# A planner's order chosen in forty rounds, zeros products in planned pauses, and kb sums copied out of PSUM

## The chip, the cores and the metric

The kernel runs on one core of one Trainium2 chip. The metric is the device time of one execution in microseconds (us). TensorE multiplies matrices, VectorE and ScalarE work element by element, GpSimd (POOL in the profile) does small jobs, SyncE (SP) issues nearly all DMAs. TensorE reads SBUF and writes PSUM, which has eight banks of 128 partitions x 512 fp32.

## The reference

Two layers (DEPTH = 2) of a decoder trunk on x of 256 tokens x 1024 channels, in fp32:

```
ada = silu(c) @ w_ada[l] + b_ada[l]                 # 6 x 1024: shift, scale, gate, twice
h   = rms_norm(x) * (1 + sc_m) + sh_m
q_a, kc, vc, ks, vs, kw, vw, g, q_b, k_b, v_b, g_br = split(h @ w_in[l])
y_a = nsa_mixer(...)      # 8 heads: compressed, selected and window attention, gated
y_b = moba_mixer(...)     # 8 heads, causal attention in blocks of 256
x  += g_m * ((sig(g_br_a) * (y_a @ w_up_nsa) + sig(g_br_b) * (y_b @ w_up_moba)) @ w_out)
h   = rms_norm(x) * (1 + sc_f) + sh_f
x  += g_f * ((silu(h @ w_gate) * (h @ w_up)) @ w_ffn_out)
```

The weights come to some 180 MB that are each read once. With 256 tokens all blocks are selected, so both mixers are causal attention beside the compressed branch.

## The kernel before, in words

**Number form.** Most weights are split on the chip: a raw block of 1 MB is landed by one DMA, ScalarE copies it to float32r (`hi`, line 444), VectorE computes `lo = raw - hi` (line 396), and TensorE does three products (x_hi w_hi, x_hi w_lo, x_lo w_hi) of 512 columns each (`mm3`, line 461). Some blocks stay whole and are multiplied in fp32. Tokens are two tiles of 128 (t = 0, 1). A sum of 512 output columns takes one PSUM bank; `dense` sums over two weight blocks into banks of the kind `acc`, of which there are three, and then calls a function that reads the sum from the bank (`post_qa`, `post_qb`, `post_kb`, `post_vb`). `post_kb` squares the sum on ScalarE, reduces the squares on VectorE, multiplies the sum by two rope tables on VectorE (each reading the bank), normalises with a power on GpSimd, and transposes.

**Stages.** The lead-in streams w_ada rows (`sa`) and w_in rows side by side, eight steps of k, while PE waits for each step's modulation. Then in each layer: `post_grpA` and the compressed branch `mlp`, q, k and v sums, attention (`nsa`, `moba`), four gate blocks, up-projections, w_out, the residual and norm of each t (`h_chain`), and the FFN.

**Modulation.** Apart from the lead-in the 80 rows of w_ada that are left (0.5 MB each, tile `aw`, three buffers) are loaded between the weights: `ada_pace(n)` is called with every weight load and draws n rows on average. Each row costs one dot product on VectorE (line 402). `ADA_PACE` holds three paces for each layer: from mlp on, from the third gate block on, in the FFN.

**The order.** Nothing is issued as it is written. Every operation becomes an `Op` with a cost for each engine that may do it; buffers are `Slot`s of a `Kind`, handed out in the order of first use. `levels` gives each op the length of the longest path behind it. `order` then simulates the engines: in each step it takes the engine that can start first and, of the ops that could start within a small window (`eps`), the one of the highest rank (level, plus a boost, plus 1000 for ops made under `R.ahead()`). DMAs are modelled at 385 bytes a ns plus 2 us. `emit` issues the instructions of all engines in that order; on the chip each engine runs its own instructions in that order and waits for semaphores. The clock of TensorE is not in the model.

Of the kernel before, what the change touches and what calls it, by code (L numbers as in the profile page):

```python
# [16 lines left out]
P = 128  # L17
# [23 lines left out]
class Cell:  # L41
    def __init__(self):
        self.busy, self.free_at = False, 0.0
# [67 lines left out]
class Op:  # L111
    def __init__(self, no, alts, key):
# [5 lines left out]
        self.func, self.loads = None, None  # L118
# [5 lines left out]
FIRST = 1000.0  # L124
LAT = {"PE": 0.24, "DVE": 0.09, "ACT": 0.09, "POOL": 0.2, "SP": 0.0, "Q": 0.0}
# [5 lines left out]
class Program:  # L131
    WAIT = 1.0
    BIAS = {"DVE": 0.8, "POOL": 0.5}
# [77 lines left out]
    def levels(self):  # L211
        for op in self.ops:
            for p in op.preds.values():
                p.succs.append(op)
# [20 lines left out]
    def order(self):  # L235
# [3 lines left out]
        for k in self.kinds.values():  # L239
            k.queue = deque(sorted((v for v in k.queue if v.ops), key=lambda v: v.first.no))  # L240
            for v in k.queue:
                v.left = v.ops
# [8 lines left out]
        ends = {}  # L251
        table = ()

        def place(op):
# [5 lines left out]
            for v in op.new:  # L260
                k = v.kind
                i = taken.get(id(k), 0)
                if len(k.queue) <= i or k.queue[i] is not v:
                    return None
                taken[id(k)] = i + 1
# [19 lines left out]
        while len(out) < len(self.ops):  # L285
# [4 lines left out]
            for op in ready:  # L290
# [5 lines left out]
                for e, (c, _) in op.alts.items():  # L296
                    est = max(free[e], pl[0],
                              max((f if q == e else f + LAT[q] for f, q in rt[op.no].values()), default=0.0))
                    per.setdefault(e, []).append((est, op, pl[1], c))
            self.done, self.ready = out, ready  # L300
            assert per, "stuck"
            for e, cs in per.items():
# [3 lines left out]
                else:  # L306
                    pick = max((c for c in cs if c[0] <= t0 + eps[e]), key=lambda c: (c[1].rank(e), -c[1].no))
# [9 lines left out]
            if len(op.alts) > 1:  # L317
# [4 lines left out]
                t = done[e] - c  # L322
            for v, s in zip(op.new, picks):
                v.kind.queue.popleft()
                v.slot, v.placed = s, True
                for cell in s.cells:
                    cell.busy = True
            if op.loads is not None:
# [15 lines left out]
            for v in op.acc:  # L344
                v.left -= 1
                v.end = max(v.end, end + LAT[e])
                if v.left == 0:
                    for cell in v.slot.cells:
                        cell.busy, cell.free_at = False, v.end
# [13 lines left out]

    def emit(self):
        for t, e, op in self.order():
# [6 lines left out]
class Engines:  # L372
# [83 lines left out]
    def mm(self, out, lhsT, rhs, start, stop, cost=None):  # L456
        if cost is None:
# [3 lines left out]
        self.p.op({"PE": (cost, [lambda: self.nc.tensor.matmul(AP(out), AP(lhsT), AP(rhs), start=start, stop=stop)])},  # L461
                  [lhsT, rhs], [out])
# [4 lines left out]
    def dma(self, out, src, q="SP"):  # L467
        o = AP(out)
        n = SIZE[o.dtype]
        for d in o.shape:  # L470
# [3 lines left out]
                  [src], [out], nbytes=max(n, 60000))  # L474
# [7 lines left out]
ADA_PACE = [(0.4, 2.5, 1.0), (0.4, 1.2, 0.6)]  # L482
# [11 lines left out]
def trunk_kernel(tc, pools, A):  # L494
# [27 lines left out]
    bc = [[Cell()] for _ in range(8)]  # L522
    for kind, ids in (("acc", (0, 1, 2)), ("s", (3, 4)), ("y", (5,)), ("t", (6, 7)), ("n", (0, 1, 2, 3, 4, 5))):
# [63 lines left out]
    zb = const("zb", [P, P], BF16)  # L587
# [33 lines left out]
    def ada_rows(l, kind, k, col):  # L621
        aw = R.val("aw")
        dma(aw, A["w_ada"][l, kind * D + k * P:kind * D + (k + 1) * P])
        ada_dot(aw, col)

    def ada_all():
        for l, nm in ((0, "g_m"), (0, "f"), (0, "g_f"), (1, "m"), (1, "g_m"), (1, "f"), (1, "g_f")):
            mod, _ = ada_tiles(l)
            if nm in ("m", "f"):
                kind = {"m": 0, "f": 3}[nm]  # L630
                for k in range(KD):
                    for j in range(2):
                        ada_rows(l, kind + j, k, mod[kind].of((j, k))[:, j, k:k + 1])
                        if (k, j) == (KD - 1, 1):
                            ada_mod(l, kind, slice(0, KD))
                        yield
# [11 lines left out]
    ada_due = [0.0]  # L648

# [16 lines left out]
    def ada_pace(n):  # L666
        ada_due[0] += n
# [67 lines left out]
    def h_rstd(t, log):  # L735
# [16 lines left out]
        else:  # L752
            ts(r, s1, 1.0 / D, b, ALU.mult, ALU.add)
            E_.raw("POOL", 1.23, lambda: nc.gpsimd.tensor_tensor(AP(r), AP(r), AP(mhalf), op=ALU.pow), [r, mhalf], [r])
# [107 lines left out]
    def consts():  # L862
        E_.raw("POOL", 0.8, lambda: make_identity(nc, AP(ident)), [], [ident])
# [6 lines left out]
    def masks():  # L870
# [3 lines left out]
        pool_memset(zb, 0.0)  # L874
# [38 lines left out]
    def lead_in(bs, h, W):  # L913
# [14 lines left out]
        dma(vecs, A["vecs"])  # L928
        load(0)
        load(1)  # L930
        dma(rows, A["rows"])
# [13 lines left out]
        for kind in (1, 4):  # L945
            ts(bT[:, :, kind], bT[:, :, kind], 1.0, None, ALU.add)
        xr = [h_norm(t, False) for t in range(NT)]
        xT = {}
        for q in range(4):
# [7 lines left out]
            evac(xT[q], b)  # L957
        R.first = False
        R.key = 4.0
# [585 lines left out]
```

## Time and profile before

| | |
|---|---|
| median of 3 runs | 846.54 us (843.9 to 848.73) |
| profiled execution | 848.27 us, of which span 846.5 us |
| mean granted TensorE clock | 0.986 |
| TensorE busy | 811.9 us (96%) |
| VectorE, ScalarE, GpSimd busy | 576.2, 418.3, 64.7 us |
| DMA | 183.82 MB, mean 217 GB/s |

The span reaches from the first to the last instruction. Busy time of TensorE counts a product from start to modelled end, also when it runs at half clock, so it is no measure of work. "Idle" before an instruction is the time for which its engine stood still ahead of it.

### The profile page before, as it was taken

The numbers are of one execution on the slowest core, as the hardware profiler recorded it, in microseconds if no ns is written. First come the engines' busy times: TensorE is split into PE (matmuls) and PEld (weight loads), VectorE is DVE, ScalarE is ACT, GpSimd is POOL, SyncE is SP. The second block draws the span as 40 slices with busy tenths as digits, with TensorE's granted clock in tenths as the row PEclk, the third lists the DMA queues.
The fourth block names the chain that finished last, engine by engine and source line by source line (L and its number), as shares of the span: only waits on it lengthen the run. The fifth ranks groups of instructions, "written<-read, shape, count | busy, mean of one in ns | idle before, by whom it ended". The sixth has DMA issues, their size and how long they took to land.

```text
span 846.5 us, 10445 instructions
## 1 busy us (share of the span) xinstructions
PE 811.9 (96%) x3948; PEld 615.9 (73%) x3948; DVE 576.2 (68%) x1008; ACT 418.3 (49%) x668; POOL 64.7 (8%) x69
## 2 busy tenths in 40 slices
PE   6998999999999999999989979999999999999996
PEld 3666756764778887888868758776557788889885
DVE  6879777777886867876778878474466644365443
ACT  5445365772672444433574445667455633354331
POOL 3603610000000000000000222000000000000000
PEclk9997999999999999999999989999999999999999
DMA  8997374658948898888848745340274555446441
GB/s 349 389 314 248 107 240 148 234 183 295 382 157 312 263 332 299 304 295 328 323 125 265 265 141 171 128 150 1 87 263 147 164 176 198 159 154 244 153 146 50
DMA packets 75349, 183.82 MB, mean 217 GB/s; under 512 B 4130, under 2 KB 9378, under 8 KB 75299
## 3 DMA queue, kind: packets, MB, share of 16 engines
q1 hardware_dynamic: 75298, 183.16, 62.2%
q8 instruction: 31, 0.51, 0.3%
q14 instruction: 20, 0.16, 0.1%
HBM read 182.10 MB, written 1.05 MB: 216 GB/s over the span
## 4 chain that ended last, share of the span: by engine, by line
PE 78%; DVE 8%; DMA 6%; ACT 4%; POOL 2%; issue 1%; SPq 0%; DVEq 0%; POOLq 0%; ACTq 0%
PE bank L461 73%; PE bank L465 5%; DVE lo L396 4%; DMA raw<-in_w_out 2%; ACT hi L444 2%; DMA rows<-in_rows 2%; DMA aw<-in_w_ada 1%; DVE tmp L396 1%; DMA raw<-in_w_ffn_in 1%; POOL tmp L396 1%; POOL tmp L414 1%; DVE tmp L414 1%; ACT hp L444 1%; DMA raw<-in_w_in 1%; DVE x L396 0%
## 5 line engine op out<-in xcount | busy, mean ns | idle before, releaser
L461 PE MATMUL bank<-hi,hp 128*128 128x512 f32 (+2 forms) x1296 | 410.7, 390 | 4.1 <-DVE tmp L396 2.1
L444 ACT ACTIVATE hi<-raw 128x2048 fp32r<-128x2048 f32 (+2 forms) x107 | 201.1, 1892 | 263.9 <-PE bank L461 204.2
L396 DVE TENSOR_TENSOR lo<-raw,hi 128x2048 fp32r<-128x2048 f32 (+2 forms) x107 | 240.1, 2261 | 121.5 <-ACT hi L444 121.0
L461 PEld LDWEIGHTS bank<-hi,hp 128*128 128x128 f32 x1296 | 241.0, 190 | 63.6 <-issue 9.3
L461 PE MATMUL bank<-lo,hp 128*128 128x512 f32 (+1 forms) x648 | 246.7, 381 | 4.6 <-DVE lo L396 4.5
L461 PEld LDWEIGHTS bank<-lo,hp 128*128 128x128 f32 x648 | 123.4, 190 | 30.8 <-DVE lo L396 6.5
L402 DVE SCALAR_TENSOR_TENSOR aw<-aw,crow 128x1024 f32<-128x1024 f32 x80 | 95.6, 1219 | 23.4 <-DMA aw<-in_w_ada 23.2
L461 PE MATMUL bank<-hi,aT 128*128 128x512 f32 x352 | 111.4, 392 | 0.0
L461 PEld LDWEIGHTS bank<-hi,aT 128*128 128x128 f32 x352 | 66.1, 188 | 13.4
L461 PE MATMUL bank<-lo,aT 128*128 128x512 f32 x176 | 68.7, 390 | 0.0
L461 PE MATMUL bank<-raw,yy 128*128 128x512 f32 x128 | 58.4, 595 | 0.8 <-ACT yy L453 0.7
L461 PE MATMUL bank<-raw,hd 128*128 128x512 f32 (+1 forms) x112 | 52.2, 597 | 1.7 <-ACT hd L444 1.6
L408 DVE CUSTOM_DVE_ANT_0 at<-bank,maskf 128x128 f32<-128x128 f32 (+1 forms) x96 | 29.8, 352 | 26.3 <-PE bank L465 21.3
L465 PE MATMUL bank<-ident,tmp 128*128 128x128 f32 x256 | 39.1, 289 | 3.9 <-ACT tmp L768 1.4
L461 PE MATMUL bank<-hi,mT 128*128 128x512 f32 x128 | 42.8, 402 | 0.0
L465 PEld LDWEIGHTS bank<-ident,tmp 128*128 128x128 f32 x256 | 32.1, 149 | 13.8 <-ACT tmp L768 2.7
L461 PEld LDWEIGHTS bank<-raw,yy 128*128 128x128 f32 x128 | 23.0, 190 | 23.2 <-issue 21.5
L461 PEld LDWEIGHTS bank<-lo,aT 128*128 128x128 f32 x176 | 33.1, 188 | 6.7 <-DVE lo L396 0.2
L444 ACT ACTIVATE at<-at,nb,rqa 128x128 f32<-128x128 f32 (+1 forms) x64 | 34.1, 536 | 3.8 <-DVE nb L402 3.8
L461 PEld LDWEIGHTS bank<-raw,hd 128*128 128x128 f32 x112 | 21.6, 201 | 19.0 <-issue 14.7
L453 ACT ACTIVATE pt<-bank 128x512 f32<-128x512 f32 x35 | 20.8, 594 | 21.7 <-PE bank L465 21.7
L732 POOL TENSOR_TENSOR r<-r,mhalf 128x4 f32<-128x4 f32 x4 | 4.1, 1020 | 355.0 <-DVE r L414 355.0
(174 smaller groups left out, 725.2 us busy)
## 6 DMA issues: line engine op xcount, KB each, us to landing
raw<-in_w_ffn_in SPq DMA_DIRECT2D x44, 1024.0 KB, 6.3
aw<-in_w_ada SPq DMA_DIRECT2D x80, 512.0 KB, 5.3
raw<-in_w_in SPq DMA_DIRECT2D x30, 1024.0 KB, 5.2
raw<-in_w_ffn_out SPq DMA_DIRECT2D x22, 1024.0 KB, 5.3
sa<-in_w_ada SPq DMA_DIRECT2D x8, 1024.0 KB, 11.0
raw<-in_w_out SPq DMA_DIRECT2D x8, 1024.0 KB, 5.5
raw<-in_w_in SPq DMA_DIRECT2D x8, 908.0 KB, 8.6
raw<-in_w_up_nsa SPq DMA_DIRECT2D x4, 1024.0 KB, 5.1
```

The costliest lines, as they stand in the source:

```text
L396: self._vec(engs, cols(out), True, lambda v: v.tensor_tensor(AP(out), AP(a), AP(b), op=op), [a, b], [out])
L402: lambda v: v.scalar_tensor_tensor(AP(out), AP(a), AP(s), AP(b), op0=op0, op1=op1, **{k: AP(x) for k, x in kw.items()}),
L408: lambda v: v.tensor_tensor_reduce(AP(out), AP(a), AP(b), 1.0, init, op0, op1, AP(accum)),
L414: lambda v: v.tensor_scalar(AP(out), AP(a), AP(s1), AP(s2), op0=op0, **kw),
L444: op = self.p.op({"ACT": (c, [lambda: self.nc.scalar.activation(AP(out), AP(a), func, **{k: AP(x) for k, x in kw.items()})])}, reads + lis ...
L453: self.p.op({"ACT": (0.17 + n / 1200, [lambda: self.nc.scalar.activation(AP(out), AP(a), AF.Copy)]), "DVE": (0.155 + n / 960, [lambda: sel ...
L461: self.p.op({"PE": (cost, [lambda: self.nc.tensor.matmul(AP(out), AP(lhsT), AP(rhs), start=start, stop=stop)])}, [lhsT, rhs], [out])
L465: self.p.op({"PE": (0.109, [lambda: self.nc.tensor.transpose(AP(out), AP(a), AP(ident))])}, [a, ident], [out])
L732: E_.raw("POOL", 1.1 + 0.13 * n, lambda: nc.gpsimd.tensor_tensor(AP(r), AP(r), AP(mh), op=ALU.pow), [r, mhalf], [r])
```

## The change

- `rounds` calls `order` forty times. After each plan `blame` looks at every pause of TensorE of 0.25 us or more after 15 us, follows back what the op after it waited for (up to 14 steps, and it stops at a TensorE op that wasn't itself waiting), and raises the boost of each op on the way by the pause, at most 3 us. The plan with the shortest span is emitted. For that each op keeps its waits, and a buffer's cell keeps who freed it.
- `fill` puts products of a block of zeros (128x128 times 128x512, bf16) into planned pauses of TensorE of 1.4 us or more, as many of 0.23 us as fit into the pause less 1.0 us, into a bank that is free in the plan. A pause that begins in the first 3 us gets eleven, planned at 0.43 us. The zeros are set first thing, on VectorE.
- The sums of kb are copied to SBUF by ScalarE (`spilled`) ahead of other work, and `post_kb` reads the copy. Only kb is listed in `SPILL`.
- The model adds 0.1 us where TensorE goes from products over part of its rows or columns to full ones or back, and looks 0.1 us further for an op of higher rank.
- `ADA_PACE` becomes (0.4, 2.5, 0.5) and (0.0, 1.2, 0.6); `modulation` draws the rows that are still missing when a norm needs them.
- In the lead-in `vecs` is loaded through GpSimd's queue, `rows` is modelled as larger, the transposed x is evacuated by ScalarE alone, and the addition of 1 to two of the biases comes after that. A power on GpSimd in `h_rstd` is planned at 0.6 instead of 1.23 us.

`LOOSE` is empty and `HOLD` is None, so what depends on them does nothing.

```diff
+    FILL, IDLE, ZERO = 1.4, 1.0, 0.23
+    FIRST_ZERO = (0.43, 11)
+    ROUNDS, WEIGHT, START = 40, 1.0, 15.0
+    SWITCH = 0.1
...
+                    if e == "PE" and op.parts != parts:
+                        est = max(est, free[e] + self.SWITCH)
...
+                    w = eps[e] + (self.SWITCH if e == "PE" else 0.0)
+                    pick = max((c for c in cs if c[0] <= t0 + w), key=lambda c: (c[1].rank(e), -c[1].no))
...
+            op.waits = [(f if q == e else f + LAT[q], self.ops[n]) for n, (f, q) in rt[op.no].items()]
+            op.waits += [(cell.free_at, cell.by) for s in picks for cell in s.cells if cell.by is not None]
...
+            if e == "PE" and self.filler:
+                f = self.fill(free[e], t)
+                if f is not None:
+                    out.append((f[0], e, f[1]))
+                    free[e] = f[0] + f[1].alts[e][0]
+                    t = max(t, free[e])
...
+    def fill(self, t0, t1):
+        z = self.zeros.val
+        if not z.placed or not z.hist or z.first.no not in self.ended:
+            return None
+        t0 = max(t0, self.ended[z.first.no] + LAT["DVE"])
+        cost, n = self.ZERO, int((t1 - t0 - self.IDLE) / self.ZERO)
+        if t0 < 3.0:
+            cost, n = self.FIRST_ZERO
+        banks = [(c.free_at, i) for i, (c, _) in enumerate(self.filler) if not c.busy]
+        if t1 - t0 < self.FILL or n < 1 or not banks:
+            return None
+        bank = self.filler[min(banks)[1]][1]
+        zs = self.zeros
+        op = Op(-1, {"PE": (n * cost, [lambda: self.nc.tensor.matmul(
+            bank.rearrange("p (a b) -> p a b", b=P), AP(zs), AP(zs)[:, None, :].to_broadcast([P, 4, P]),
+            start=True, stop=True)] * n)}, 0.0)
...
+    def blame(self):
+        to, end = {}, 0.0
+        for op in sorted((o for o in self.ops if o.placed[1] == "PE"), key=lambda o: o.placed[0]):
+            t, e, c = op.placed
+            gap, end = t - end, t + c
+            if gap < 0.25 or t < self.START:
+                continue
+            seen = set()
+            while op is not None and len(seen) < 14 and op.no not in seen:
+                seen.add(op.no)
+                to[op.no] = max(to.get(op.no, 0.0), min(gap, 3.0))
+                ready, by = max(op.waits, key=lambda w: w[0], default=(0.0, None))
+                if by is not None and by.placed[1] == "PE" and len(seen) > 1 and ready < op.placed[0] - 0.3:
+                    break
+                op = by
+        return to
+
+    def rounds(self):
+        best = None
+        for i in range(self.ROUNDS):
+            self.order()
+            if best is None or self.span < best[0] - 1e-9:
+                best = (self.span, [op.boost for op in self.ops])
+            to = self.blame()
+            for op in self.ops:
+                op.boost += self.WEIGHT * to.get(op.no, 0.0)
+        for op, b in zip(self.ops, best[1]):
+            op.boost = b
+        return self.order()
...
-ADA_PACE = [(0.4, 2.5, 1.0), (0.4, 1.2, 0.6)]
+SPILL = [("kb",), ("kb",)]
+SPILL_FIRST = True
+HOLD = None
+ADA_PACE = [(0.4, 2.5, 0.5), (0.0, 1.2, 0.6)]
...
+    def modulation(l, nm):
+        while nm + "_done" not in ada.get(l, {}):
+            next(ada_it)
+        return ada[l]["A_" + nm], ada[l]["sh_" + nm]
...
-        dma(vecs, A["vecs"])
+        dma(vecs, A["vecs"], q="POOL")
...
-            evac(xT[q], b)
+            act(xT[q], b, AF.Copy)
...
+        def spilled(post, spots):
+            def go(t, b):
+                v, i = spots[t]
+                q = quarter(v, i, i)
+                R.stage = f"{l}post"
+                with R.ahead(SPILL_FIRST):
+                    act(q, b, AF.Copy)
+                post(t, q)
+            return go
...
-        dense(1816, 512, post_kb)
+        dense(1816, 512, spilled(post_kb, SP["kb"]) if "kb" in SPILL[l] else post_kb)
```

## Rows read from the trace of the kernel before

**Rows 1.** The page's first two sections: busy time, share of the span and instructions of each engine; and TensorE's granted clock in 40 equal slices of 21.2 us, in tenths of full speed.
```profile
PE 811.9 (96%) x3948; PEld 615.9 (73%) x3948; DVE 576.2 (68%) x1008; ACT 418.3 (49%) x668; POOL 64.7 (8%) x69
...
PEclk9997999999999999999999989999999999999999
```

**Rows 2.** The table of busy time by stretch. Columns: start and end of the stretch in us, its length; then busy us (and instructions) of TensorE, its weight loads, VectorE, ScalarE and GpSimd; granted clock as a share; mean busy share of the DMA engines; GB/s.
```profile
62.40:82.20 19.80, 15.41 (x114) 11.89 (x112) 18.46 (x31) 11.04 (x17) 7.09 (x5) 0.74 0.70 243
...
190.00:251.00 61.00, 58.06 (x242) 38.79 (x241) 50.08 (x71) 33.31 (x48) 0.00 (x0) 1.00 0.78 280
251.00:430.00 179.00, 177.84 (x860) 149.14 (x858) 134.80 (x147) 76.18 (x68) 0.00 (x0) 1.00 0.84 297
430.00:446.00 16.00, 12.83 (x52) 9.24 (x51) 12.93 (x28) 12.55 (x26) 0.00 (x0) 0.89 0.51 155
...
468.00:490.00 22.00, 20.37 (x151) 16.23 (x151) 19.89 (x31) 8.20 (x11) 5.34 (x2) 1.00 0.81 266
490.00:503.00 13.00, 7.66 (x25) 5.39 (x25) 10.57 (x23) 5.40 (x12) 2.08 (x2) 0.74 0.47 159
503.00:603.00 100.00, 100.00 (x565) 73.09 (x565) 60.30 (x193) 66.50 (x156) 7.54 (x5) 1.00 0.32 106
603.00:660.00 57.00, 54.43 (x228) 36.64 (x227) 35.87 (x47) 30.30 (x41) 0.00 (x0) 1.00 0.49 168
...
837.00:846.50 9.50, 2.86 (x14) 2.03 (x12) 5.08 (x8) 0.80 (x2) 0.00 (x0) 0.82 0.29 110
```

**Rows 3.** The list of TensorE's waits: who waited for whom, us in total, how many times, the longest in us.
```profile
PE bank L461 <- DVE lo L396: 6.7, 6, 1.4
...
PE bank L461 <- DVE tmp L396: 1.7, 1, 1.7
PE bank L461 <- ACT vbd L444: 1.7, 1, 1.7
...
PE bank L465 <- DVE kbd_tok L414: 1.5, 1, 1.5
```

**Rows 4.** The table by stretch for TensorE alone: stretch, length, TensorE's busy us (and instructions), granted clock, DMA share, GB/s.
```profile
62.40:68.20 5.80, 2.58 (x44) 1.00 0.58 220
68.20:78.40 10.20, 9.02 (x59) 0.50 0.73 256
...
436.84:440.25 3.41, 3.41 (x10) 0.50 0.40 120
494.87:501.70 6.83, 4.63 (x11) 0.50 0.49 154
```

**Rows 5.** The timeline of the lead-in: start us, length us (of the merged instructions together), engine, line, operation, tiles, count; in brackets the idle time before, and what ended it.
```profile
11.35 0.69 DVE L454 COPY pt<-bank 128x512 f32<-128x512 f32 x1
...
14.32 9.37 PE L461 MATMUL bank<-raw,hd 128*128 128x512 f32 x16 [1.62 <-ACT hd L444]
...
17.11 1.72 ACT L444 ACTIVATE hi<-raw 128x1816 fp32r<-128x1816 f32 x1 [2.40 <-DMA raw<-in_w_in]
...
20.82 0.48 DVE L396 TENSOR_TENSOR hp<-hd,hp 128x256 fp32r<-128x256 f32 x1
...
27.39 4.92 PE L461 MATMUL bank<-raw,hd 128*128 128x512 f32 x12
```

**Rows 6.** The timeline around 495 us, same columns. The last row is the first product of the sum that waited for a bank.
```profile
491.06 0.40 PE L461 MATMUL bank<-hi,hp 128*128 128x512 f32 x1
...
493.51 0.60 ACT L444 ACTIVATE tmp<-bank 128x512 f32<-128x512 f32 x1
...
496.44 0.60 ACT L444 ACTIVATE tmp<-bank 128x512 f32<-128x512 f32 x1 [0.92 <-DVE ss L422]
...
496.92 0.68 DVE L396 TENSOR_TENSOR tmp<-bank,st 128x512 f32<-128x512 f32 x1
...
497.65 0.79 PE L461 MATMUL bank<-hi,hp 128*128 128x512 f32 x1 [2.12 <-DVE tmp L396]
```

**Rows 7.** The table by stretch for the instructions on the tiles aw alone (the w_ada rows): stretch, length, busy us of VectorE (and instructions; each dot product is one instruction and one read of the accumulator, so two), the same of ScalarE, clock, DMA share, GB/s.
```profile
251.00:430.00 179.00, 48.87 (x82) 0.00 (x0) 1.00 0.84 297
...
430.00:490.00 60.00, 11.88 (x20) 0.00 (x0) 0.97 0.74 238
```

**Rows 8.** VectorE's timeline at 318 us, columns as in rows 5.
```profile
318.07 1.23 DVE L402 SCALAR_TENSOR_TENSOR aw<-aw,crow 128x1024 f32<-128x1024 f32 x1 [4.80 <-DMA aw<-in_w_ada]
...
319.22 2.29 DVE L396 TENSOR_TENSOR lo<-raw,hi 128x2048 fp32r<-128x2048 f32 x1
```

**Rows 9.** The groups of instructions, shapes kept apart: line, engine, operation, tiles out<-in, partitions x elements, count, busy us, mean ns of one, and idle us before them with what ended it.
```profile
L461 PE MATMUL bank<-zb,identb 128*128 128x512 bf16 x4 | 1.7, 433 | 1.7 <-ACT vbd L444 1.7
...
L453 ACT ACTIVATE pt<-bank 128x512 f32<-128x512 f32 x35 | 20.8, 594 | 21.7 <-PE bank L465 21.7
...
L402 DVE SCALAR_TENSOR_TENSOR aw<-aw,crow 128x1024 f32<-128x1024 f32 x80 | 95.6, 1219 | 23.4 <-DMA aw<-in_w_ada 23.2
...
L396 DVE TENSOR_TENSOR tmp<-bank,ct 128x512 f32<-128x512 f32 x10 | 6.8, 683 | 1.7 <-ACT tmp L444 1.7
...
L396 DVE TENSOR_TENSOR tmp<-e,ct 128x512 f32<-128x512 f32 x2 | 1.4, 684 | 0.0
```

**Rows 10.** The page's DMA issues: tile and tensor, queue, operation, count, KB each, median us from issue to landing.
```profile
aw<-in_w_ada SPq DMA_DIRECT2D x80, 512.0 KB, 5.3
```

More of the change, by code (lines that the diff above doesn't have):

```diff
@@ L117, in __init__ @@
         self.stage, self.first, self.boost = None, False, 0.0
-        self.func, self.loads = None, None
+        self.func, self.loads, self.parts = None, None, False
     def rank(self, e):
@@ L239, in order @@
         for k in self.kinds.values():
-            k.queue = deque(sorted((v for v in k.queue if v.ops), key=lambda v: v.first.no))
-            for v in k.queue:
-                v.left = v.ops
+            k.queue = []
+            for s in k.slots:
+                for c in s.cells:
+                    c.busy, c.free_at, c.by = False, 0.0, None
+        for v in self.allvals:
+            if v.ops:
+                v.left, v.end, v.placed = v.ops, 0.0, False
+                v.kind.queue.append(v)
+        for k in self.kinds.values():
+            k.queue = deque(sorted(k.queue, key=lambda v: v.first.no))
         self.levels()
@@ L250, in order @@
         eps = {"PE": 0.08, "DVE": 0.05, "ACT": 0.05, "POOL": 0.05, "SP": 0.0, "Q": 0.0}
-        ends = {}
+        ends = self.ended = {}
         table = ()
+        parts = False
         def place(op):
@@ L262, in place @@
                 i = taken.get(id(k), 0)
+                taken[id(k)] = i + 1
                 if len(k.queue) <= i or k.queue[i] is not v:
-                    return None
-                taken[id(k)] = i + 1
+                    if sum(not c.busy for s in k.slots for c in s.cells) - i <= LOOSE.get(v.name, 99):
+                        return None
                 best = None
@@ L348, in order @@
                     for cell in v.slot.cells:
-                        cell.busy, cell.free_at = False, v.end
+                        cell.busy, cell.free_at, cell.by = False, v.end, op
             ready.remove(op)
@@ L460, in mm, with dma @@
             cost = (4 * n / 2400 + 0.006) if full else n / 2400 + 0.0135
-        self.p.op({"PE": (cost, [lambda: self.nc.tensor.matmul(AP(out), AP(lhsT), AP(rhs), start=start, stop=stop)])},
-                  [lhsT, rhs], [out])
+        op = self.p.op({"PE": (cost, [lambda: self.nc.tensor.matmul(AP(out), AP(lhsT), AP(rhs), start=start,
+                                                                    stop=stop)])}, [lhsT, rhs], [out])
+        op.parts = AP(lhsT).shape[0] < P or AP(out).shape[0] < P
     def tr(self, out, a, ident):
         self.p.op({"PE": (0.109, [lambda: self.nc.tensor.transpose(AP(out), AP(a), AP(ident))])}, [a, ident], [out])
-    def dma(self, out, src, q="SP"):
+    def dma(self, out, src, q="SP", least=60000, late=()):
         o = AP(out)
@@ L522, in trunk_kernel @@
     bc = [[Cell()] for _ in range(8)]
+    R.filler = [(c[0], b) for c, b in zip(bc, banks)]
     for kind, ids in (("acc", (0, 1, 2)), ("s", (3, 4)), ("y", (5,)), ("t", (6, 7)), ("n", (0, 1, 2, 3, 4, 5))):
@@ L666, in ada_pace @@
     def ada_pace(n):
+        if ada_held[0] and "g_m_col" in ada.get(1, {}):
+            return
         ada_due[0] += n
```

56 lines of the change are left out of this document (38 added, 18 removed).

## The prediction

> **What bounds the kernel now.** I read the page first. TensorE is busy for 811.9 of 846.5 us, and its granted clock is full in nearly every slice [rows 1]. So it is the bound, and what can be won is what it loses: pauses, and stretches at half clock. The table of busy time by stretch [rows 2] says where the pauses lie (length less PE busy): 4.39 us in 62.4:82.2 (from the lead-in to the first layer), 2.94 in 190:251 (up-projections and w_out), 1.16 in 251:430, 3.17 in 430:446 (layer change), 1.63 in 468:490, 5.34 in 490:503, 2.57 in 603:660. In 503:603 there is none, so that nothing can be won there. Together 21.2 us; the 9.5 us of the tail hold the last residual and store, which the change doesn't touch. The list of TensorE's waits names who ended the pauses: mostly VectorE (lo halves of weight splits, products) [rows 3]. These are waits on an order, since VectorE as a whole is not full.
>
> Then the clock. TensorE was granted 1.2 instead of 2.4 GHz in 68.2:78.4, 436.84:440.25 and 494.87:501.70, each time right behind pauses; it worked 9.02, 3.41 and 4.63 us in them [rows 4], half of which, 4.5 + 1.7 + 2.3 = 8.5 us, is lost. At the start the row shows full clock, but the times don't: 16 records raw,hd last 9.37 us where 12 later ones last 4.92 [rows 5]; at that pace 16 would last 6.6, so 2.8 us are lost. 8.5 + 2.8 = 11.3 us.
>
> Besides the start-up's pauses, at most 21.2 + 11.3 = 32.5 us are to be had.
>
> **The change part by part**, each with gain and bounds.
>
> Lead-in (to 62.4). The third and fourth evacuation of transposed x go to ScalarE alone: a VectorE copy of 0.69 us leaves the space between the two w_ada dot products that the first matmul waits for [rows 5]; vecs leaves SP's queue, one issue of 0.43 us ahead of sa and raw. Eleven zeros products in the first microseconds are meant to lift the clock: 11 x 0.433 us (the mean of the four products zb has now [rows 9]) = 4.8 us from about 1 us on. They push the ones products back by some 1.5 us; the dot product at 10.2 us, which needs crow, hides that just so, and beyond it each us is lost. If the clock is up at 14.3, k=0 ends 2.8 us sooner; but k=1 (split) waits for its hi, whose weights landed only at 17.1 (2.40 us of waiting for the DMA), and for hp lo, ready at 20.82 + 0.48 = 21.3, not 23.1 [rows 5]. So 1.8 us is the end. I take 1.0 for the clock and 1.0 for the copy and the issue: 2.0 (bounds -1.5 to 4).
>
> 62.4:82.2. VectorE is busy 18.46 of 19.8 us [rows 2]: no order makes it faster, and raw buffers come free only with the lead-in's end. So of 4.39 us of pause I take 1.0. Zeros fill a pause planned at 1.4 us or more up to its last microsecond; the longest here is 1.74 [rows 3], so few products. Of the 4.5 us of clock I take 3.0. Sum 4.0 (0 to 8).
>
> 190:251 and 603:660. Same work in both layers: 2.94 and 2.57 us. The rounds raise whatever a PE pause is traced back to, by up to 3 us a round, and forty of them can turn lo products forward. But w_out is loaded only when raw buffers come free. I take half of the first, 1.5, and 1.0 of the second (-2 to 4 together).
>
> 251:430. VectorE does 82/2 = 41 w_ada dot products here [rows 7], 41 x 1.22 = 50 us, and the pause of 1.16 us has its cause in one: VectorE, in order, waited 4.80 us for a w_ada row with a lo product behind it [rows 8]. The pace goes from 1.0 to 0.5 row per load over 33 loads: 16.5 rows fewer. I take 1.1 (0 to 1.5).
>
> 430:490. The 20/2 = 10 w_ada products here [rows 7] fall to about 3 (pace 0.5 for six loads, then 0). Of 3.17 us of pause 1.5, of 1.7 of clock 1.0, of 1.63 in 468:490 1.0: 3.5 (0 to 6.5).
>
> 490:503, the clearest place. TensorE waits 2.12 us for a sum's bank, after 1.50 (kbd_tok) and 1.72 (vbd) us. Three sums (both of qb, the first of kb) sit in the three acc banks; ScalarE squares the first at 493.51 and the third at 496.44, VectorE's rope products read them behind a lo product, and the first bank is free at 497.6 [rows 6]. The change copies a kb sum to SBUF ahead of other ScalarE work: 0.59 us (PSUM copies of that shape [rows 9]). The first kb sum ends at 491.06 + 0.40 [rows 6], so its bank is free at about 492, 5.5 us sooner; the weights for the second kb sum are long there. Costs: four such copies in the kernel, 2.4 us of ScalarE, busy 5.40 of 13 us here [rows 2]; the rope products cost the same from SBUF (684 ns) as from PSUM (683) [rows 9]. What is late next is kbd_tok and vbd, small, with kb products to cover them. I take 4.0 of 5.34 and 2.0 of the clock's 2.3: 6.0 (2 to 7.6).
>
> Against it. A zeros run is planned; where the chip pauses less than planned, it stands in PE's order ahead of real work at 0.23 us each (full clock). Five runs with one and a half products too many: 1.7 us (0 to 5). The w_ada rows come later: from paces and loads I count 33 by layer 0's w_out, 50 by its end, 53 after six loads more, then 1.2 for each of 12 loads from the third gate block on, and five that layer 1's FFN norm asks for at once. So some 20 rows, 24.4 us of VectorE, move into 560:660, where VectorE is busy 35.87 of 57 us from 603 on [rows 2] and has room; layer 0 does the same with pauses alike. I put 0.9 (0 to 12). Sum -2.6.
>
> The planner's new costs (pow, rows, a switch of PE's parts) change only the order, which is in the terms above: nothing, -2 to 2.
>
> Total: 2.0 + 4.0 + 2.5 + 1.1 + 3.5 + 6.0 - 2.6 = 16.5 us. Span 846.5 - 16.5 = 830.0; the profiled execution took 848.27, 1.8 us more than its span, and 1.7 more than the median of 846.54, so on the median the forecast is also 846.5 - 16.5 = **830.0 us**.
>
> A rule that speaks against a part of it: the Trainium skill, "TensorE: Matmul & The Clock Gate", section "Part 1: The HAM clock gate", holds the ramp to be worth less than 1% of a typical span and variable from run to run, and advises not to fit to it. By that the clock terms would be under 8.5 us and not to be counted on. This trace shows 11.3 us, 1.3%, of which I count 7.0; the rule's case is the second rival below.
>
> **The rivals.**
> - The rounds buy nothing on the chip: each plan is as far from the chip as the last, and new pauses come for old ones. For it: the waits of 0.2 to 2 us [rows 3] are as small as a DMA's spread (w_ada rows land in 5.3 us in the middle [rows 10], and one came 4.80 late). Left are the kb copy 4.0, w_ada's 1.1, the lead-in's 1.0 and the clock's 7.0, less 2.6 and about 3 of new waits: 7.5, 839.
> - The clock stays where it is: a few zeros in a pause that keeps its last microsecond don't hold 2.4 GHz. For it: in 62.40:68.20 TensorE worked 2.58 of 5.80 us and the clock fell all the same [rows 4]. Against: in 490:503 the pauses themselves should go. Without the 7.0: 837.
> - More is won: three quarters of the 32.5 us, 24.4, and nothing lost, since splits can be pulled forward wherever ScalarE and VectorE have room (VectorE is free for 44 of the 179 us of 251:430 [rows 2]): 822.
> - Slower: the late w_ada rows. VectorE works in order, so a dot product whose row hasn't landed holds every lo product behind it, as at 318 us [rows 8]. Layer 1's FFN norm asks for five rows at once, through three buffers: two landings of 5.3 us and a product of 1.2, 11.8 us of pause, then 10.2 us at half clock like 68.2:78.4 (4.5 lost [rows 4]): 16.3. At the layer change the 48th row is due about three loads before the end; if it lands late, 5.3 + 4.5 = 9.8. Both: 830 + 26 = 856. It decides from 20.7 us on; one alone (846) does not. Against it: the rows are asked for in program order, ahead of the FFN's weights, and the DMA engines are busy only half of 603:660 [rows 2].
> - The change doesn't do what it says: the first of the forty plans is the best one, and the order differs only by the other edits. Same remains as in the first rival: 839.
>
> **How the numbers follow.** Forecast (823 to 836, at 830) 0.50; first, second and last rival (836 to 842.3) 0.22; more (below 823) 0.15; a mixture that ends within 0.5% (842.3 to 850.8; 0.5% is what a measurement of this kernel can tell from no change) 0.07; the slower rival 0.06. Faster 0.87, same 0.07, slower 0.06. For 8 in 10 I leave out 6 in 100 below 817 and the slower tenth above 843: 817 to 843.
>
> **What would show it.** After the change the profile should show: granted clock full in the slices at 63 to 85 and 490 to 505 us; no wait of TensorE above 1 us around the second kb sum; new ScalarE copies into ve ahead of the squares; some 25 w_ada dot products instead of 41 in layer 0's FFN, and about 20 after layer 1's third gate block; products zb beyond the present six, and next to none of them directly ahead of products that were ready. TensorE's idle time should fall from 34.6 to about 22 us. It would be wrong if that idle time stays (first rival), if the clock's low stretches stay at 20 us (second), or if VectorE's waits for w_ada grow beyond the present 23.4 us [rows 9] and TensorE's waits follow at 640 to 660 us.

## The result and the profile after

834.85 us (median of 4 runs, 833.42 to 836.11) against 846.97 us for the kernel before, measured beside it: a ratio of 0.986, 95% interval 0.982 to 0.990, so 12 us or 1.4% faster. The forecast was 830.0, with 817 to 843 as its range. The profiled execution after took 833.42 us (span 831.5), that of before 848.27 (846.5). The two spans lie 15.0 us apart, some 3 us more than the medians: the profiled run of before lay 1.3 us above its median, that of after 1.4 us below. What follows explains these 15.0 us.

Each trace is one execution, and TensorE's clock differs between executions of one kernel. In 56 of before, measured beside the experiments, its mean granted clock lay between 0.984 and 0.992; the seven at 0.992 took 843.7 us in the mean, the eight at 0.986 (that of the profiled run) 847.8. So a piece of 3 or 4 us in one stretch can be the luck of a run, where the clock is part of it.

The page after (answers to [rows 1]), TensorE's busy time and its granted clock in 40 slices, and the group of the zeros products from the list of groups:

```profile
PE 810.5 (97%) x3983; PEld 612.0 (74%) x3983; DVE 578.0 (70%) x1014; ACT 419.9 (50%) x667; POOL 66.1 (8%) x69
...
PEclk9999999999999999999999999999999999999999
...
L415 PE MATMUL bank<-zb 128*128 128x512 bf16 x35 | 11.4, 483 | 1.1 <-DVE zb L692 1.1
```

TensorE seems to stand still for 831.5 - 810.5 = 21.0 us instead of 34.6. That is not so: 11.4 us of the busy time are zeros, which multiply nothing of use. With them counted as pauses it is 32.4 (at most: a product's modelled end can overlap the next). A filler raises the busy share and hides the pauses from whoever reads only this line.

To see where the 15.0 us came from, I divided both traces at the same work: at TensorE's last product of the lead-in, of layer 0's compressed scores, its w_out, its FFN, layer 1's compressed scores, its w_out, and the end. Columns as in [rows 2]; the third number is the stretch's length, the one after it TensorE's busy time. Before:

```profile
0.00:60.67 60.67, 54.02 (x175) 33.47 (x176) 45.54 (x91) 28.48 (x48) 22.91 (x42) 1.00 0.94 349
60.67:133.43 72.76, 68.37 (x344) 47.14 (x343) 58.86 (x138) 37.70 (x84) 24.83 (x17) 0.93 0.64 219
133.43:238.44 105.01, 103.44 (x533) 68.89 (x533) 80.43 (x194) 61.18 (x124) 0.00 (x0) 1.00 0.67 234
238.44:430.91 192.47, 189.94 (x910) 157.64 (x909) 146.92 (x169) 87.77 (x91) 0.00 (x0) 1.00 0.82 288
430.91:548.28 117.37, 107.13 (x569) 84.71 (x569) 88.60 (x186) 63.89 (x122) 16.99 (x10) 0.96 0.59 192
548.28:650.22 101.94, 100.23 (x526) 67.50 (x525) 59.78 (x152) 59.93 (x122) 0.00 (x0) 1.00 0.36 125
650.22:846.50 196.28, 188.76 (x900) 156.59 (x899) 96.05 (x82) 79.34 (x79) 0.00 (x0) 0.99 0.46 161
```

After:

```profile
0.00:56.54 56.54, 53.64 (x182) 31.43 (x183) 42.33 (x88) 27.54 (x46) 21.28 (x41) 0.97 0.90 351
56.54:129.83 73.29, 69.22 (x363) 47.33 (x363) 59.85 (x143) 39.33 (x88) 22.86 (x16) 0.98 0.68 228
129.83:235.27 105.44, 104.21 (x536) 68.95 (x535) 79.51 (x192) 59.06 (x120) 1.29 (x1) 1.00 0.63 218
235.27:429.12 193.85, 191.19 (x913) 158.03 (x913) 147.89 (x171) 87.74 (x89) 0.00 (x0) 1.00 0.81 286
429.12:535.69 106.57, 103.84 (x575) 82.77 (x574) 89.82 (x186) 64.22 (x120) 19.32 (x11) 1.00 0.68 226
535.69:636.40 100.71, 100.14 (x523) 66.90 (x522) 63.56 (x156) 62.75 (x128) 1.30 (x1) 1.00 0.42 142
636.40:831.50 195.10, 188.29 (x900) 156.57 (x899) 95.00 (x83) 79.23 (x77) 0.00 (x0) 0.99 0.45 156
```

Length by length: -4.1 in the lead-in, +0.5, +0.4 and +1.4 in the rest of layer 0 (so all of layer 0 nets 1.8), **-10.8** in the first half of layer 1, -1.2 and -1.2 behind it. One stage carries most of the gain. In it the pauses (length less TensorE's busy time) fell from 10.2 to 2.7 us, or 3.3 with its zeros, and the 4.0 us that before lost to half clock at 437 and 495 us [rows 4] are gone.

**Layer 0 gave back over half of what the lead-in won.** The timelines, before and then after, columns as in [rows 5]: ScalarE's first split behind the lead-in, and what TensorE did there.

```profile
66.91 1.93 ACT L444 ACTIVATE hi<-raw 128x2048 fp32r<-128x2048 f32 x1 [2.36 <-DMA raw<-in_w_in]
```

```profile
61.77 2.11 PE L415 MATMUL bank<-zb 128*128 128x512 bf16 x9
...
67.85 1.91 ACT L533 ACTIVATE hi<-raw 128x2048 fp32r<-128x2048 f32 x1 [5.65 <-DMA raw<-in_w_in]
...
70.46 0.57 PE L550 MATMUL bank<-sel,at 128*128 128x60 f32 x2 [3.09 <-ACT at L533]
```

The lead-in ends 4.1 us sooner. Part of that is work which the new order puts behind it: without the 19 zeros, 163 products lie in the first stretch instead of 175, and without the 11 zeros 352 instead of 344 in the second. The first whole block of w_in landed no sooner than before: its split starts at 67.85 instead of 66.91 us. ScalarE waits 5.65 us for it, and since it works in order, the small copy `at` (70.14 us) that the compressed branch's matmul needs stands behind that split: a new pause of 3.09 us. Pauses in 56.54:129.83 come to 73.29 - 69.22 = 4.07 us, plus 2.54 us of zeros (eleven from 61.3 us on): 6.6 against 4.4 before. The half-clock stretch there fell from 10.2 to 3.4 us in return, so the stretch kept its length to within 0.5 us.

Why did the block land no sooner? It was not asked for later: its DMA was issued at 58.51 us, 2.2 us ahead of before (60.70). But the DMA engines had stood almost idle ahead of it, before and then after, columns as in [rows 2]:

```profile
50.00:54.00 4.00, 4.00 (x15) 2.38 (x14) 1.38 (x1) 2.63 (x3) 0.00 (x0) 1.00 1.01 380
```

```profile
50.00:54.00 4.00, 4.00 (x14) 2.30 (x13) 4.00 (x6) 0.26 (x1) 0.00 (x0) 1.00 0.24 53
```

SyncE waited 7.1 us for TensorE there, to issue the load of the compressed branch's key weights (51.42 us; 47.15 before), and two w_ada rows and the block came behind it. That is the likely reason; no run tests it. The block is not all that sets the end of this stretch, though: in run 11 below its split starts at 63.52 us, and yet the compressed scores end at 130.92 us, against 129.83 in after. What else does is open.

**In layer 0's FFN the w_ada rows didn't move.** The same view as [rows 7], for a stretch that covers the same part of layer 0's FFN; and VectorE's timeline that answers to [rows 8]:

```profile
248.00:428.00 180.00, 48.87 (x82) 0.00 (x0) 1.00 0.84 298
```

```profile
316.07 1.22 DVE L491 SCALAR_TENSOR_TENSOR aw<-aw,crow 128x1024 f32<-128x1024 f32 x1 [5.67 <-DMA aw<-in_w_ada]
```

82 instructions, 41 dot products, before and after; and the wait for the one late row is still there, 5.67 instead of 4.80 us. In layer 1 some did move: after first, then before (where 430:490 held ten dot products, [rows 7]):

```profile
430.00:490.00 60.00, 7.35 (x12) 0.00 (x0) 1.00 0.76 256
490.00:603.00 113.00, 9.71 (x16) 0.00 (x0) 1.00 0.39 126
```

```profile
490.00:603.00 113.00, 0.06 (x2) 0.00 (x0) 0.97 0.34 112
```

Six instead of ten, and eight instead of none. The new paces did not do that: with the old ones put back into after, the planner writes the very same program for all five engines. It is the order of the other work.

**Layer 1's pauses went.** TensorE's list of waits after, answering to [rows 3]:

```profile
PE bank L550 <- DVE lo L485: 5.2, 5, 1.5
PE bank L550 <- ACT at L533: 3.1, 1, 3.1
...
PE bank L550 <- DVE tmp L485: 1.0, 1, 1.0
...
PE bank L555 <- DVE kbd_tok L503: 0.5, 1, 0.5
```

The waits for lo halves are nearly as long as before (5.2 against 6.7 us); what fell are the waits of layer 1: the bank of the second kb sum (2.1) is no longer waited for, `vbd` (1.7) is gone, `kbd_tok` fell from 1.5 to 0.5.

### The profile page after: what moved, and what is told of

Its sections match the earlier page's. It is cut to its first block, busy times and chain, and to the rows that moved or that the text cites. A ratio compares the mean times of both kernels' runs of the same rounds, so it can differ in the third digit from the quotient of the medians.

```text
span 831.5 us, 10528 instructions
## 1 busy us (share of the span) xinstructions
PE 810.5 (97%) x3983; PEld 612.0 (74%) x3983; DVE 578.0 (70%) x1014; ACT 419.9 (50%) x667; POOL 66.1 (8%) x69
## 4 chain that ended last, share of the span: by engine, by line
PE 77%; DVE 8%; DMA 8%; ACT 3%; issue 2%; POOL 2%; SPq 0%; DVEq 0%; POOLq 0%; ACTq 0%
PE bank L550 72%; PE bank L555 5%; DVE lo L485 4%; DMA aw<-in_w_ada 2%; DMA raw<-in_w_in 2%; ACT hi L533 2%; DMA rows<-in_rows 1%; DVE tmp L485 1%; DMA raw<-in_w_ffn_in 1%; DMA raw<-in_w_out 1%; POOL tmp L485 1%; DVE tmp L503 1%; POOL tmp L503 1%; DVE aw L491 1%; ACT hp L533 1%
## 5 line engine op out<-in xcount | busy, mean ns | idle before, releaser
L485 DVE TENSOR_TENSOR lo<-raw,hi 128x2048 fp32r<-128x2048 f32 (+2 forms) x107 | 243.0, 2286 | 122.6 <-ACT hi L533 122.4
L550 PE MATMUL bank<-lo,hp 128*128 128x512 f32 (+2 forms) x648 | 244.9, 378 | 4.2 <-DVE lo L485 4.0
L491 DVE SCALAR_TENSOR_TENSOR aw<-aw,crow 128x1024 f32<-128x1024 f32 x80 | 95.8, 1219 | 24.6 <-DMA aw<-in_w_ada 24.4
L550 PE MATMUL bank<-raw,hd 128*128 128x512 f32 (+1 forms) x112 | 49.1, 568 | 0.0
L550 PEld LDWEIGHTS bank<-raw,yy 128*128 128x128 f32 x128 | 23.2, 190 | 26.2 <-issue 23.4
L485 POOL TENSOR_TENSOR tmp<-tmp,tmp 128x512 f32<-128x512 f32 (+1 forms) x9 | 11.7, 1296 | 219.1 <-DVE tmp L491 212.6
L550 PEld LDWEIGHTS bank<-hi,mT 128*128 128x128 f32 x128 | 24.0, 188 | 5.7 <-DVE mT L491 0.6
```

The costliest lines, as they stand in the source:

```text
L485: self._vec(engs, cols(out), True, lambda v: v.tensor_tensor(AP(out), AP(a), AP(b), op=op), [a, b], [out])
L491: lambda v: v.scalar_tensor_tensor(AP(out), AP(a), AP(s), AP(b), op0=op0, op1=op1, **{k: AP(x) for k, x in kw.items()}),
L550: op = self.p.op({"PE": (cost, [lambda: self.nc.tensor.matmul(AP(out), AP(lhsT), AP(rhs), start=start, stop=stop)])}, [lhsT, rhs], [out])
```

## The experiments

"After" and "before" are the two kernels; every ratio is to before, measured beside it, with its 95% interval. The **planner's own count** is the span that `order` finds and the rounds make small. With the switch price in it, it is 814.4 us for after; for before it is 823.0, without the price.

**1. Do the rounds carry it?** After with one plan:

```diff
-    ROUNDS, WEIGHT, START = 40, 1.0, 15.0
+    ROUNDS, WEIGHT, START = 1, 1.0, 15.0
```

> The changed kernel with ROUNDS = 1: the first plan is emitted, all other edits stay. The planner's own span is 829.9 us for this plan, 814.4 for the best of forty and 823.0 for the kernel before. If the rounds carry the gain and the plan's differences come through on the chip, this kernel takes 12 to 16 us more than the changed one: 847 to 851 us, no faster than before. If the rounds buy nothing on the chip and zeros, lead-in and the kb copy carry the gain: 833 to 837 us. In between, 840 to 843, both have a part.

846.93 us, 1.001 [0.999, 1.003]. With one plan all other edits together are worth nothing that shows. The rounds turn 847 into 835.

**2. The rounds alone.** Before with the rounds: no kb copy, no zeros, no switch price, the lead-in as before. As an edit of after (the pace edit, which does nothing, as told above, stays in here and in the kernels made from this one):

```diff
-    SWITCH = 0.1
+    SWITCH = 0.0
...
-            if e == "PE" and self.filler:
+            if False:
...
-SPILL = [("kb",), ("kb",)]
+SPILL = [(), ()]
...
-        dma(vecs, A["vecs"], q="POOL")
+        dma(vecs, A["vecs"])
...
-            act(xT[q], b, AF.Copy)
+            evac(xT[q], b)
```

> The kernel before with the forty rounds alone: no zeros, no copy of kb, no price on a switch of PE's parts, the lead-in as before. Its plan takes 812.8 us by the planner's count, 10.2 less than the kernel before's 823.0 by the same count. If the rounds alone carry the gain: 834 to 837 us. If they need the other edits, the price on a switch above all: 839 to 844 us.

835.19 us, 0.989 [0.987, 0.992]: 9 to 10 of the 12 us (by the ratio or the medians), with none of the other ideas. What these add in after is not clear of the noise: the two intervals overlap. The stretch that gained 10.8 us in after, the first half of layer 1, gained 11.7 here:

```profile
428.24:533.88 105.64, 103.14 (x572) 82.63 (x572) 89.68 (x187) 64.04 (x122) 17.17 (x10) 1.00 0.65 213
```

One thing that the rounds did there can be read from ScalarE's timeline, before and then here: the squares of the compressed keys (`sqc`), from which `kbd_tok` follows, come 59.8 us behind the start of that stretch before and 47.7 us here. ScalarE's next three squares of a whole bank, which before were crowded at 493.51, 494.92 and 496.44 us, are spread over 477.95, 483.45 and 489.06.

```profile
490.75 0.22 ACT L444 ACTIVATE sqc<-bank 64x64 f32<-64x64 f32 x1 [6.61 <-PE bank L461]
```

```profile
475.93 0.22 ACT L533 ACTIVATE sqc<-bank 64x64 f32<-64x64 f32 x1 [1.66 <-PE bank L550]
```

**3. The kb copy alone.** The kernel of 2 with one plan and the copies:

```diff
-    ROUNDS, WEIGHT, START = 40, 1.0, 15.0
+    ROUNDS, WEIGHT, START = 1, 1.0, 15.0
...
-SPILL = [(), ()]
+SPILL = [("kb",), ("kb",)]
```

> The kernel before with the copies of the kb sums alone, planned once; the planner's span is 822.3 instead of 823.0 us. By the prediction's term, the copy frees the bank 5.5 us sooner and TensorE's pauses around 495 us with the fall of the clock go: 840 to 843 us. If the copy alone only moves the wait to another sum or another read: 845 to 848 us.

839.52 us, 0.993 [0.991, 0.996]: 5.7 us. Where they come from, TensorE's table over the same work (layer 1, from the end of the compressed branch's first products to the end of the up-projections; columns as in [rows 4]), in before, then here, then in the kernel of 2:

```profile
473.50:624.37 150.87, 144.86 (x736) 0.98 0.40 132
```

```profile
470.52:616.63 146.11, 143.82 (x735) 1.00 0.40 136
```

```profile
467.08:608.99 141.91, 141.49 (x732) 1.00 0.45 151
```

The pause falls from 6.01 to 2.29 us by the copy and the clock stays full: 4.8 us of length, of 7.8 between the two profiled runs; the other 3.0 lie in layer 0, beside a low stretch behind the lead-in of 3.4 us in place of 10.2. In the kernel of 2 it falls to 0.42 us **without a copy**: with the order of the rounds TensorE no longer waits there. The two edits cure the same pause, so their gains don't add (run 4).

**4. After without the copy** (planned anew):

```diff
-SPILL = [("kb",), ("kb",)]
+SPILL = [(), ()]
```

> The changed kernel without the copies of the kb sums (SPILL empty), planned again in forty rounds; the planner's best span is 817.3 instead of 814.4 us. If the copy is what took the pauses out of 490 to 503 us: 839 to 841 us, with pauses of TensorE of some 4 us or more ahead of the second kb sum. If the rounds take them out by order alone: 834 to 838 us and no such pause.

838.53 us, 0.989 [0.984, 0.993]. Some 2 to 4 us are lost (by the ratios or the medians), less than the 5.7 that the copy is worth alone and not clear of the noise (832.68 to 840.34). And they are not lost where the copy acts: the first half of layer 1 is as short without it (106.57 us in after), and what is longer is layer 0, which ends at 433.75 instead of 429.12 us.

```profile
433.75:539.03 105.28, 103.14 (x571) 82.21 (x571) 89.46 (x187) 64.32 (x123) 16.11 (x10) 1.00 0.66 219
```

**5. After without the zeros**, in the order of after: the products are planned but not issued. They reach no output.

```diff
         for t, e, op in self.rounds():
+            if op.stage == "fill":
+                continue
```

> The changed kernel's order with no zeros product issued; everything else stays in the same order. If the zeros are there for the clock and do hold it: the first products run at half clock again (2.8 us), the clock falls again around 65 us for some 10 us (3 us more than now) and at 432 us (1.7 us): 840 to 843 us. If the clock would have stayed up without them in the new order, or they cost as much as they bring: 833 to 836 us.

833.28 us, 0.985 [0.982, 0.987]: the same as after, if anything faster. The clock, TensorE's table over its low stretch at 70 us, after and then here:

```profile
70.62:74.03 3.41, 3.41 (x12) 0.50 1.05 401
```

```profile
70.13:73.54 3.41, 3.17 (x10) 0.50 1.05 403
```

and the first 16 products of the lead-in, again after and then here (9.37 us before, [rows 5]):

```profile
13.56 6.26 PE L550 MATMUL bank<-raw,hd 128*128 128x512 f32 x16
```

```profile
13.58 6.36 PE L552 MATMUL bank<-raw,hd 128*128 128x512 f32 x16 [1.32 <-ACT hd L535]
```

In this order the clock falls for as long and at the same place, and the first products are as fast, with or without 11.4 us of zeros.

**6. The zeros on the order of before.** The kernel of 2 with one plan and the zeros:

```diff
-            if False:
+            if e == "PE" and self.filler:
...
+        pool_memset(zb, 0.0, "DVE")
...
-        pool_memset(zb, 0.0)
```

> Before with the zeros products alone: one plan, no kb copy, the lead-in as before (except that the zeros are set first, on VectorE), no switch price. Theory 'zeros don't hold the clock and cost little': within 2 us of before, about 845 to 848, with the low stretches at 68, 437 and 495 us still there. Rival, the prediction's: up to 7.0 us of clock won, 839 to 841, with full clock in 68 to 78 and 495 to 502.

846.9 us, 1.000 [0.998, 1.002]: nothing. TensorE's clock in its low stretches:

```profile
14.82:18.23 3.41, 3.41 (x7) 0.50 1.00 407
72.84:76.26 3.42, 3.42 (x10) 0.50 1.05 402
496.10:499.51 3.41, 3.41 (x10) 0.50 0.47 118
```

The stretches at 68 and 495 us of [rows 4] have become shorter (10.2 to 3.4 and 6.8 to 3.4) and that at 437 is gone, yet the time is the same. Here the zeros did raise the clock: its mean is 0.993 to 0.995 in all ten runs, above every run of before (0.984 to 0.992). What that won went into pauses: less its 18.7 us of zeros TensorE's busy time is 800.7 us instead of 811.9, and pauses and zeros together take 45.9 instead of 34.6 (ends that overlap make both differences some 3 us too large). Whether the zeros held up real work or the faster products waited longer for other engines, the runs don't separate.

**7. The lead-in alone:** the kernel of 2 with one plan and all the lead-in's edits:

```diff
+        pool_memset(zb, 0.0, "DVE")
...
-        dma(vecs, A["vecs"])
+        dma(vecs, A["vecs"], q="POOL")
...
-            evac(xT[q], b)
+            act(xT[q], b, AF.Copy)
```

> The kernel before with the lead-in's edits alone (vecs by GpSimd's queue, transposed x by ScalarE alone, zb first, the cost of the power), planned once; the planner's span is 823.1 instead of 823.0 us. If the 4 us by which the changed kernel ends its lead-in earlier come from these edits and last to the end: 842 to 844 us. If they are waited away afterwards, in the wait for the first weights behind the lead-in: 845 to 848 us.

844.12 us, 0.999 [0.997, 1.002]: nothing that is clear of the noise.

**8. What eats the copy's gain in run 1?** There the copy was in, and yet it gave 846.9 and not 839.5. Two suspects: the zeros, and the switch price. Run 1 without its zeros:

```diff
         for t, e, op in self.rounds():
+            if op.stage == "fill":
+                continue
```

> After with one plan in place of forty, and with the zeros products planned but not issued (they reach no output). It is the run with one plan (846.9 against 846.2 before) without its 13.1 us of zeros. Theory 'zeros are worth nothing in either order': 845 to 848, as with forty plans, where leaving them out gave 833.3 against 834.9. Rival 'in an order with many small pauses the zeros stand ahead of real work and cost': 840 to 843, since the run with the kb copy alone gave 839.5. If it stays at 846, what eats the copy's 5 to 6 us is the order that the switch price makes, and the next run but one should show that.

846.43 us, 1.000 [0.997, 1.002]: not the zeros. (In this order they did quicken the first 16 products, 6.26 us with them and 7.83 without, and no time came of it.) The kernel of 2 with one plan and the switch price:

```diff
-    SWITCH = 0.0
+    SWITCH = 0.1
```

> Before with the planner's price of 0.1 us for a switch between products over a part of TensorE and full ones, and nothing else: one plan, no zeros, no kb copy. The planner's own span, counted without the price, is worse by some 6 us than without the price. Theory 'the price is what eats the kb copy's gain in the run with one plan': 850 to 853, slower than before by 4 to 7 us. Rival 'the price makes the order truer to the chip': 840 to 845.

854.86 us, 1.009 [1.007, 1.011]: 8 us slower than before, more than expected. One pause from its list of waits, which is 1.5 us in [rows 3]:

```profile
PE bank L555 <- DVE kbd_tok L503: 4.7, 1, 4.7
```

The rest of the 8 us lies mostly in layer 0, which ends at 434.43 instead of 430.91 us. Run 1 without its zeros shows both: layer 0 ends at 434.27 us, and the stretch of run 3 is short as with the copy alone:

```profile
478.45:623.94 145.49, 143.24 (x736) 1.00 0.38 132
```

So -5.7 for the copy and +8 for the price, with nothing for the rest, is run 1's zero to within 2 or 3 us. With rounds the price loses nothing:

**9. After without the price** (forty rounds, planned anew, `SWITCH = 0.0`):

> The changed kernel without the price on a switch of PE's parts and the wider window (SWITCH = 0), planned again in forty rounds (816.4 us by a count without that price, against 812.8 for the rounds alone on the kernel before). If that price matters on the chip: 838 to 842 us, with more of the small pauses where products over part of the rows alternate with full ones. If not: 833 to 837 us.

838.33 us, 0.993 [0.990, 0.995]: 3 to 6 us slower than after (by the medians or the ratios). So the price costs with one plan, and of these two searches the one with it found the faster kernel; but the rounds alone, without the price, gave 835.2 (run 2). What an edit of the planner gives in one plan says little of what it gives after a search; whether the price or chance made after's plan the better one, two searches can't tell.

**10. Fewer rounds.** After with `ROUNDS = 9`, which leaves a plan of 817.1 us in place of 814.4:

> The changed kernel with ROUNDS = 9: another plan, whose own span is 817.1 us, 2.7 more than the best. If the chip follows the plan's differences: 836 to 839 us. If plans this close to one another are not told apart by the chip, anywhere from 831 to 843 us, and then the choice of the tenth plan is luck.

838.1 us, 0.990 [0.987, 0.993]: 2.7 us more by the planner, 3.3 more on the chip, with overlapping intervals. The plan of after is the tenth of the forty, and none of the thirty behind it is shorter: the search doesn't close in on a good plan, it comes upon one.

**11. A version that should beat both:** no zeros, no price, sixty rounds with more weight.

```diff
-    ROUNDS, WEIGHT, START = 40, 1.0, 15.0
+    ROUNDS, WEIGHT, START = 60, 1.5, 15.0
...
-    SWITCH = 0.1
+    SWITCH = 0.0
...
-            if e == "PE" and self.filler:
+            if False:
```

> After with no zeros, no switch price, and sixty rounds with weight 1.5 in place of forty with 1.0. The plan's span, counted without the price, is 813.4 us against 814.4 (which has the price in it) for after. Theory 'the chip follows the plan by 18 to 20 us': 831 to 834, at or just under after. Rival 'the plan of after is one of a chance kind that suits the chip, and a plan without the price loses at the switches': 835 to 839, as the run with the price at nothing gave 838.3.

837.41 us, 0.989 [0.987, 0.991]. A miss: the plan is 1.0 us shorter than that of after and the kernel 2.6 us slower. The best kernel measured is that of run 5, after without its zeros, and its lead over after (833.28 to 834.85) is within the spread.

The planner's count beside the chip's median:

| kernel | planner, us | chip, us | chip less planner |
|---|---|---|---|
| switch price alone | 832.7 | 854.9 | 22.2 |
| after, one plan | 829.9 | 846.9 | 17.0 |
| lead-in alone | 823.1 | 844.1 | 21.0 |
| before | 823.0 | 846.5 | 23.5 |
| kb copy alone | 822.3 | 839.5 | 17.2 |
| after without the copy | 817.3 | 838.5 | 21.2 |
| after, nine rounds | 817.1 | 838.1 | 21.0 |
| after | 814.4 | 834.9 | 20.5 |
| sixty rounds, run 11 | 813.4 | 837.4 | 24.0 |
| rounds alone | 812.8 | 835.2 | 22.4 |

The chip follows the planner with some 17 to 24 us on top. So ten us off the plan show on the chip, and two or three alone don't decide which kernel is faster. The two kernels with the smallest difference are one-plan kernels with the copy; why, I didn't find out.

## Why the prediction was right, and which of its steps were not

The forecast was 16.5 us and the change gave 12 (15.0 between the profiled runs). The sum held because one large term was right and others missed in both directions, and in part by luck: 6.0 us were put down to the kb copy and 7.0 to a clock that zeros would lift, and the rounds alone gave 9 to 10 of the 12 us with neither (run 2).

- **430:490 and 490:503, 3.5 + 6.0 forecast, 10.8 found.** Right in place and size. The kb copy was priced at 4.0 us of pause and 2.0 of clock; alone it removed 3.7 us of pause, and its stretch became 4.8 us shorter (run 3). What was missed is that the rounds don't need the copy for it (runs 2 and 4). The 3.5 rested in part on w_ada products falling from ten to three by the pace; they fell to six, and not by the pace.
- **Lead-in, 2.0 forecast, 4.1 found; then 62.4:82.2, 4.0 forecast, -0.5 found.** This step failed. It took the pauses and the clock of that stretch as losses to be won, as if the work there could move. The clock was won in the profiled run (10.2 us of low stretch became 3.4), but pauses and zeros rose from 4.4 to 6.6 us, 3.09 of them behind the landing of the first block of w_in, and eight more products lay in the stretch. ScalarE's wait of 2.36 us for that block stood in the trace of before (shown above); I had not read it. How much of the 4.1 in the lead-in is the edits' is not shown either: run 7, with the lead-in's edits alone, is not measurably faster than before.
- **190:251 and 603:660, 2.5 forecast.** -0.4 found in layer 0 (133:238) and +1.2 in layer 1 (548:650). Too high by half and more; the lo products' waits barely fell.
- **251:430, 1.1 forecast, -1.4 found.** The step "the pace goes from 1.0 to 0.5 row per load: 16.5 rows fewer" failed: no row fewer, and the same late row; the pace edit does nothing, as told above. My reading of the code is that a row's DMA is placed as soon as one of three `aw` buffers is free, wherever the program asks for it; that was not tried on the chip.
- **Against it, -2.6 forecast.** No cost found. Of the 20 rows that were to move into 560:660, eight moved behind 490 us, and the last w_ada dot product lies ahead of 592.5 us. VectorE's waits for w_ada rows came to 24.4 us instead of 23.2. The zeros cost 0 to 1.6 us (run 5).
- **The clock terms, 7.0.** They came, but not from zeros: the loss at half clock in the stretches of [rows 4], 8.5 us, fell to 1.7 at 70 us, with a new low stretch in the lead-in (9.18 to 12.59 us), where zeros are part of the work; and it did so in run 5 without zeros too (3.17 us of work at half clock at 70 us, and no other low stretch before the tail). In layer 1, where the pauses had ended with VectorE's work and not with a load [rows 6], clock became time; in the stretch behind the lead-in of after it did not.

The rule weighed in the prediction, from the Trainium skill, "TensorE: Matmul & The Clock Gate", "Part 1: The HAM clock gate", not to fit to the clock's ramp because it is small and varies, is borne out for the start: the first 16 products took 9.37 us before, 8.05 with zeros added to it (run 6) and 6.36 with no zeros in after's order (run 5); run 6, 1.3 us quicker there than before, took as long as before in all. The clock that falls again in mid-kernel is another thing than this ramp: in layer 1 the 4.0 us lost to half clock went with the pauses and came off the time.

The rivals. "The rounds buy nothing" and "the first plan is the best" are refuted by run 1 against after. "The clock stays" had the wrong size (837) and a right core: no time came from zeros. As it was worded, that they don't hold the clock, it fits run 5; in run 6 they did raise it. "More is won" did not happen. "Late w_ada rows" did not happen: few rows moved, and TensorE didn't wait for them. Of the signs that I named, TensorE's idle time fell to 21.0 us as forecast (22), and that sign was a bad one: it counts 11.4 us of zeros as work.

## What to carry to other kernels

When a program is ordered by a planner, let it try many orders: here that alone was worth 9 to 10 us, and an edit that cures one pause by hand added nothing clear of the noise beside it. Before pricing a pause, ask what else its stage waits for: behind the lead-in, time won on the clock came back as waits. Before reading 3 us out of one trace, look at the mean clock of the kernel's other runs. Count filler products out of the busy time before reading it.

## What the runs showed that I had not expected

- Zeros products in pauses did nothing measurable to the time in three pairs: 834.9 with and 833.3 without, 846.9 and 846.4, 846.9 and 846.7 (before). In after, eleven of them ran between 61.3 and 64 us, and the clock was at half from 70.62 on all the same.
- Less half clock need not be less time: run 6 spent 10.2 us in low stretches before its tail where before spent 20.5 ([rows 4]), at the same 847 us. And yet among before's own runs, in one and the same order, the higher clock goes with the shorter time (843.7 us at 0.992, 850.3 at 0.984).
- A planner's price of 0.1 us for a switch between partial and full products made the kernel 8 us slower in one plan; after forty plans the kernel with it was 3 to 6 us faster than the one without, one search each.
